# Mixer phase of a hybrid decoder layer: gate rows requested one slice earlier, the last cached weight units kept out of the raw slots, one more slice for the scan

## The chip, the cores and the metric

The kernel runs on one core of a Trainium2 chip, as a single program. Its time is the device time of one execution in microseconds (us), given as the median of several runs. In the profile PE is TensorE (PEld its weight loads), DVE VectorE, ACT ScalarE, POOL GpSimd and SP SyncE; a "q" behind a name is that engine's DMA queue.

## What is computed

One inference step of a decoder layer in float32: a prompt of 2048 tokens and 8 single-token samples, model width 1024. Cut to what matters here:

```python
h = _rmsnorm(x, g_norm1) * (1 + scale1) + shift1
proj = h @ w_in                                  # pool | q k v | z | b a | glu
y_a = _pool_mixer(pool_ext, pos0, pool_w, pool_scale)
qkv = silu(_causal_dwconv(qkv_ext, qkv_conv_w))  # then split; q, k normalised per head
beta = sigmoid(proj[..., OFF_B:OFF_A])
g = -exp(a_log) * softplus(proj[..., OFF_A:OFF_GLU] + dt_bias)
o, s_new = _gated_delta(q, k, v, beta, g, s0)    # chunked: inverse within a chunk, scan over chunks
y_b = rmsnorm(o) * dn_norm_g * silu(z)
y_c = silu(layernorm(_causal_dwconv(glu))) @ conf_pw_w
x = x + gate1 * (concat([y_a, y_b, y_c]) @ w_out)
a = relu((_rmsnorm(x, g_norm2) * (1 + scale2) + shift2) @ w_ff1)
x = x + gate2 * ((a * a) @ w_ff2)                # then a final rmsnorm
```

Returned are the outputs for prompt and samples, and the states of the pool, the two convolutions and the delta rule.

## The kernel before

**Arithmetic.** Matrix products are made from a high and a low part of each operand: `unit_mm` (L172 to 182) adds hi x hi, hi x lo and lo x hi, over eight steps k of 128 rows, so 24 matmuls for one unit (a block of 128 columns of a weight against 512 tokens). The weight's parts are called `whi` and `wlo`, the activation's `hhi` and `hlo`.

**Phases.** First the mixer, then the feed-forward network (L1571 and L1805 are its matmuls). The mixer goes over four groups of 512 tokens. Each group has 22 units of `w_in`, in the order glu (4), pool (2), z0, z1, k (4), v (4), q (4), z2, z3: units 0 to 87 in all. The last group carries the samples too, so that its units are made in two column parts of 260. Behind them come 32 out-projection units, in which the roles are turned: the columns of `y_scr` (the mixer's output, in DRAM) are the weight, and `w_out` is the activation. `load_w` (L1098) fetches its tiles `wt`, casts them to `hhi` on ScalarE (L1109) and subtracts to get `hlo` (`split_lo`, L132) on VectorE or, each few times, on GpSimd.

**Weights.** `load_raw` (L134) fetches a unit into one of two slots with the tag "raw" (L139, on ScalarE's queue). `load_unit` (L142) casts it to `whi` on ScalarE (L151) and makes `wlo` with `split_lo`; both have slots with tags of their own. In group 0 the parts of each `w_in` unit are also written to DRAM (`w_scr`), and in the later groups `load_cached` (L157) only reads both back (L169). Since no raw tile is needed then, every third of these units is put into the two raw slots, in place of a whi and a wlo slot, by a counter `wnum` (L166): unit 86 gets whi and wlo, unit 87 raw and raw. The out-projection units go through `load_unit`. In the job loop (L1303) the weights of a unit are requested three units ahead.

**Delta rule.** For each group, `gates` (L640) computes the decay sums and writes them as rows to `g_scr` (L668); `delta_prep` (L672) reads them back, spread over the partitions, as `Gb` (L678), twice eight heads and chunks, and makes tails and decay matrices from them (L681 to 690). `delta_inverse` solves the triangular systems (L751 and L752 are its substitution on VectorE, L772 its first product). `delta_scan` (L817) does the part within a chunk (`within`, L827 to 830) for two halves, then four chunk steps (`chunk`) and the normalisation (`finish`).

**Order.** These routines are generators: each `yield` ends a slice, and the job loop lets every one that is under way make one slice per unit (`tick`). That is the order in which the program is written. The order on each engine is then made by the framework's scheduler, which takes instructions by priority (program order, moved by `tc.high_priority`) and a simulated time at which they are ready; the slots of a pool decide how early a load can be.

Of the kernel before, what the change touches and what calls it, by code (L numbers as in the profile page):

```python
# [17 lines left out]
P = 128  # L18
# [44 lines left out]
def hybrid_trunk(  # L63
# [13 lines left out]
    w_ada, w_in, w_out, w_ff1, w_ff2 = w_ada[0], w_in[0], w_out[0], w_ff1[0], w_ff2[0]  # L77
# [49 lines left out]
    wcount, lo_share, wnum = [1], [LS], [0]  # L127
# [26 lines left out]

    w_scr = {}

    def load_cached(key, src, early=None):  # L157

        if key not in w_scr:
            hi, lo = load_unit(src, early)  # L160
            w_scr[key] = dram.tile([2, P, D], F32, name=f"w_scr{key}")
            for i, v in enumerate((hi, lo)):
                nc.sync.dma_start(out=w_scr[key][i], in_=v.bitcast(F32).rearrange("p k m -> p (k m)"))
            return hi, lo
        wnum[0] += 1
        tags = (("whi", "wlo"), ("raw", "raw"), ("whi", "wlo"))[wnum[0] % 3]  # L166
        out = tuple(wp.tile([P, KT, P], F32R, tag=t, name=n) for t, n in zip(tags, ("whi", "wlo")))
        for i, v in enumerate(out):
            wq[0].dma_start(out=v.bitcast(F32).rearrange("p k m -> p (k m)"), in_=w_scr[key][i])  # L169
        return out  # L170
# [70 lines left out]
    with ExitStack() as ph1:  # L241
# [26 lines left out]
        early = tc.high_priority(offset=30000)  # L268
# [403 lines left out]
        def delta_prep(g, st):  # L672

            V, A = nc.vector, nc.scalar
            for hf in range(2):
                Gt = st['Gt'][:, hf * 8:hf * 8 + 8]
                Gb = d4.tile([P, 8, P], F32, tag="Gb", name="Gb")
                nc.sync.dma_start(out=Gb, in_=g_scr[g, hf * 8:hf * 8 + 8, :].partition_broadcast(P))  # L678
                eGl = sm.tile([P, 8], F32, tag=f"eGl{hf}", name="eGl")
                tail = sm.tile([P, 8], F32, tag=f"tail{hf}", name="tail")  # L680
                V.tensor_tensor(out=tail, in0=Gb[:, :, P - 1], in1=Gt, op=ALU.subtract)  # L681
                A.activation(out=tail, in_=tail, func=AF.Exp)
                A.activation(out=eGl, in_=Gb[:, :, P - 1], func=AF.Exp)
                QK = d4.tile([P, 8, P], F32, tag="QK", name="QK")
                for i in range(8):
                    V.scalar_tensor_tensor(out=QK[:, i, :], in0=Gb[:, i, :], scalar=Gt[:, i:i + 1], in1=mneg,
                                           op0=ALU.subtract, op1=ALU.min)
                A.activation(out=QK, in_=QK, func=AF.Exp)
                A.activation(out=Gb, in_=Gb, func=AF.Exp)
                st['dec'].append((Gb, QK, eGl, tail))  # L690
                yield
# [125 lines left out]
        def delta_scan(g, st):  # L817
# [61 lines left out]
            within(0)  # L879
            yield  # L880
            within(1)
            chunk(0, 0, osq[0])
            yield
            chunk(0, 1, osq[0])
# [292 lines left out]
        w_ready = [load_cached(c, w_in[:, c:c + P], d4 if i in EARLY else None) for i, c in enumerate(first_jobs)]  # L1177
# [75 lines left out]
        for g in range(NG):  # L1253
            st = {'dec': [], 'inv': []}
# [37 lines left out]
        for q, tiles in OP_PLAN:  # L1292
            jobs.append((None, q, {}, "load_w"))
            for tt in tiles:
# [3 lines left out]
                if tt >= 12 and first_last is None:  # L1298
                    first_last = sum(j[0] is not None for j in jobs)
                jobs.append((y_scr[:, tt * P:(tt + 1) * P], 0, {},  # L1300
                             lambda g, st, pss, tt=tt, q=q, done=done: op_unit(pss[0], tt, q, done)))

        w_jobs = [j[0] for j in jobs if j[0] is not None]  # L1303
        wi = len(w_ready)
        scan = inv = smp = None
        for src, g, st, what in jobs:
            if src is not None:
                if wi == first_last:
                    finish_all(scan)
                if wi < len(w_jobs):  # L1310
                    nxt = w_jobs[wi]
                    w_ready.append(load_cached(nxt, w_in[:, nxt:nxt + P]) if isinstance(nxt, int) else load_unit(nxt))
                    wi += 1
                w = w_ready.pop(0)
                if wi >= len(w_jobs) - len(op_tiles) or wi == len(w_jobs):
# [604 lines left out]
```

## Time and profile before

| | us |
|---|---|
| median of 3 runs (2493.01 to 2502.81) | 2496.91 |
| the profiled execution | 2489.5 |
| its span, from first to last instruction | 2487.8 |
| TensorE busy (94%) | 2340.6 |
| VectorE busy (76%) | 1892.3 |
| ScalarE busy (44%) | 1093.8 |
| GpSimd busy (28%) | 692.1 |
| TensorE's own part of the chain that ended last | 30% of the span |

The page gives busy time by engine; what an engine waited for is in the rows of the timeline, where a bracket holds the idle time before an instruction and what ended it. TensorE's matmuls overlap, so their starts, not their durations, tell the pace: the distance between two starts is what one costs. The granted clock is the share of the full 2.4 GHz that TensorE was given; 0.50 is the lower level, 1.2 GHz.

### The profile page before, as it was taken

What the parts mean: (1) busy time and instruction counts of PE and PEld (TensorE: products, weight loads), DVE (VectorE), ACT (ScalarE), POOL (GpSimd) and SP (SyncE); (2) the same over time, 40 slices, a digit from 0 to 9 for tenths busy, and PEclk for the clock granted to TensorE, in tenths of its full rate; (3) what the DMA queues carried; (4) which work ended last, traced back from release to release, by engine and by line L of the source; (5) the groups of instructions that cost most, each with busy time, mean ns of one, the idle gap of its engine ahead of it and who ended that gap; (6) DMA issues with size and microseconds to landing.
All of it is one profiled execution on the core that took longest, in us unless ns stands there. A gap on an engine that the chain in (4) does not pass through costs nothing. (4 is left out here: it accounts for less than half of the span.)

```text
span 2487.8 us, 36542 instructions
## 1 busy us (share of the span) xinstructions
PE 2340.6 (94%) x12797; PEld 1879.6 (76%) x12797; DVE 1892.3 (76%) x3378; ACT 1093.8 (44%) x2411; POOL 692.1 (28%) x469
## 2 busy tenths in 40 slices
PE   7989999999999999989999999999989999999991
PEld 3567788788999788667777767777668888888881
DVE  3986987887887586677878796767777787777767
ACT  3266247237336443455575675555532221221205
POOL 2101101011111234543237332323431223231324
PEclk9999999999999999999999999999999999999996
DMA  9976434544643567854779785656675555556553
GB/s 328 360 272 223 171 136 163 179 142 158 213 139 124 153 196 222 269 172 132 241 228 333 239 273 171 191 173 185 212 253 163 167 166 167 170 158 180 162 161 146
DMA packets 456327, 490.73 MB, mean 197 GB/s; under 512 B 40106, under 2 KB 364395, under 8 KB 456120
## 3 DMA queue, kind: packets, MB, share of 16 engines
q1 hardware_dynamic: 381296, 386.55, 48.5%
q10 hardware_dynamic: 73088, 96.48, 11.8%
q0 software_dynamic: 1760, 5.38, 0.7%
q8 instruction: 101, 1.65, 0.3%
q14 instruction: 82, 0.67, 0.1%
HBM read 335.63 MB, written 153.07 MB: 196 GB/s over the span
## 5 line engine op out<-in xcount | busy, mean ns | idle before, releaser
L180 PE MATMUL ps_ip<-hhi,whi 128*128 128x512 f32 (+1 forms) x1112 | 410.6, 370 | 11.4 <-ACT whi L151 9.2
L180 PE MATMUL ps_ip<-hhi,wlo 128*128 128x512 f32 (+1 forms) x1112 | 408.7, 368 | 8.4 <-DVE wlo L132 8.1
L180 PE MATMUL ps_ip<-hlo,whi 128*128 128x512 f32 (+1 forms) x1112 | 407.8, 367 | 4.4 <-DVE hlo L132 3.3
L180 PEld LDWEIGHTS ps_ip<-hhi,whi 128*128 128x128 f32 x1112 | 211.0, 190 | 53.2 <-ACT whi L151 10.8
L180 PEld LDWEIGHTS ps_ip<-hhi,wlo 128*128 128x128 f32 x1112 | 210.9, 190 | 48.5 <-DVE wlo L132 12.0
L180 PEld LDWEIGHTS ps_ip<-hlo,whi 128*128 128x128 f32 x1112 | 210.7, 190 | 38.7 <-DVE hlo L132 5.2
L1780 ACT CAST ai<-ai 128x512 fp32r<-128x512 f32 (+1 forms) x128 | 72.3, 567 | 350.0 <-DMA ai<-a_scr 334.4
L1805 PE MATMUL ps_v<-wo,ai 128*128 128x512 f32 x768 | 197.6, 391 | 2.4 <-DVE wo L1399 1.9
L1805 PE MATMUL ps_z<-wo,ai 128*128 128x512 f32 x768 | 197.0, 391 | 2.3 <-DVE wo L1399 1.5
L1805 PE MATMUL ps_x<-wo,ai 128*128 128x512 f32 x768 | 195.3, 395 | 1.7 <-DMA ai<-a_scr 1.7
L1571 PE MATMUL ps_v<-xo,wo 128*128 128x512 f32 x744 | 186.2, 397 | 7.3 <-DVE t L1396 5.2
L552 DVE SCALAR_TENSOR_TENSOR dc<-glu,dww,dc 128x512 f32<-128x512 f32 x240 | 189.3, 816 | 1.7
L1399 DVE TENSOR_TENSOR wo<-s,wo 128x512 fp32r<-128x512 f32 x128 | 122.5, 962 | 84.5 <-ACT wo L1402 83.4
L1571 PE MATMUL ps_x<-xo,wo 128*128 128x512 f32 x744 | 185.5, 397 | 1.0 <-ACT s L1612 0.7
L1571 PE MATMUL ps_z<-xo,wo 128*128 128x512 f32 x744 | 183.2, 394 | 0.3 <-DVE t L1396 0.3
L1402 ACT CAST wo<-raw 128x512 fp32r<-128x512 f32 x192 | 116.5, 619 | 152.3 <-POOL raw L1399 41.1
L1687 POOL TENSOR_TENSOR raw<-raw,g 128x1024 f32<-128x1024 f32 x32 | 84.2, 2653 | 353.1 <-DMA ai<-a_scr 282.6
L1399 DVE TENSOR_TENSOR ai<-ai 128x512 fp32r<-128x512 f32 (+1 forms) x128 | 100.8, 789 | 104.9 <-ACT ai L1780 104.6
L1805 PEld LDWEIGHTS ps_x<-wo,ai 128*128 128x128 f32 x768 | 145.5, 190 | 38.3 <-DVE acc L1396 3.3
L1571 PEld LDWEIGHTS ps_v<-xo,wo 128*128 128x128 f32 x744 | 137.8, 188 | 43.3 <-DVE t L1396 8.0
L1805 PEld LDWEIGHTS ps_z<-wo,ai 128*128 128x128 f32 x768 | 144.3, 188 | 33.8 <-DVE wo L1399 2.3
L1805 PEld LDWEIGHTS ps_v<-wo,ai 128*128 128x128 f32 x768 | 144.2, 188 | 33.6 <-DVE wo L1399 2.9
(507 smaller groups left out, 4774.6 us busy)
## 6 DMA issues: line engine op xcount, KB each, us to landing
a_scr<-ae SPq DMA_DIRECT2D x112, 512.0 KB
raw<-in_w_ff SPq DMA_DIRECT2D x94, 512.0 KB
whi<-w_scr ACTq DMA_DIRECT2D x66, 512.0 KB
wlo<-w_scr ACTq DMA_DIRECT2D x66, 512.0 KB
ai<-a_scr SPq DMA_DIRECT2D x64, 512.0 KB
mraw<-in_w_ada SPq DMA_DIRECT2D x48, 512.0 KB
ai<-a_scr SPq DMA_DIRECT2D x64, 384.0 KB
a_scr<-s SPq DMA_DIRECT2D x80, 256.0 KB
```

Source lines behind the costliest of these rows:

```text
L180: nc.tensor.matmul(out=ps, lhsT=a[:, k, :], rhs=b, start=(i == 0), stop=(i == 3 * KT - 1))
L552: nc.vector.scalar_tensor_tensor(out=d, in0=gt[:, j:j + GT], scalar=dww[:, t, j:j + 1], in1=d, op0=ALU.mult, op1=ALU.add)
L1399: eng.tensor_tensor(out=out, in0=in0, in1=in1, op=ALU.subtract)
L1402: A.copy(out=entry[:, 0, :], in_=full)
L1571: nc.tensor.matmul(out=ps, lhsT=w[:, a, c], rhs=x[:, b, :], start=start and i == 0, stop=stop and i == 2, skip_group_check=True)
L1687: Q.tensor_tensor(out=raw, in0=raw, in1=g2, op=ALU.mult)
L1780: A.copy(out=e[:, :, 0, :], in_=e32[:, :, 1, :])
L1805: nc.tensor.matmul(out=ps, lhsT=a[q][n // 4][:, n % 4, x, :], rhs=w[q][r][:, y, :], start=first and q == 0 and i == 0, stop=last and q == ...
```

## The change

Three edits. (1) `delta_prep` issues both loads of `Gb` in its first slice, ends the slice, and computes from the second slice on; it has three slices now in place of two. (2) `load_cached` takes a flag `last`; with it a unit always takes whi and wlo slots. The job loop sets it for the last two `w_in` units, 86 and 87. (3) `delta_scan` ends a slice between `within(1)` and `chunk(0, 0)`, so that it has one slice more.

```diff
--- before.py
+++ after.py
@@ -154,7 +154,7 @@
 
     w_scr = {}
 
-    def load_cached(key, src, early=None):
+    def load_cached(key, src, early=None, last=False):
 
         if key not in w_scr:
             hi, lo = load_unit(src, early)
@@ -163,7 +163,7 @@
                 nc.sync.dma_start(out=w_scr[key][i], in_=v.bitcast(F32).rearrange("p k m -> p (k m)"))
             return hi, lo
         wnum[0] += 1
-        tags = (("whi", "wlo"), ("raw", "raw"), ("whi", "wlo"))[wnum[0] % 3]
+        tags = (("whi", "wlo"), ("raw", "raw"), ("whi", "wlo"))[0 if last else wnum[0] % 3]
         out = tuple(wp.tile([P, KT, P], F32R, tag=t, name=n) for t, n in zip(tags, ("whi", "wlo")))
         for i, v in enumerate(out):
             wq[0].dma_start(out=v.bitcast(F32).rearrange("p k m -> p (k m)"), in_=w_scr[key][i])
@@ -672,10 +672,14 @@
         def delta_prep(g, st):
 
             V, A = nc.vector, nc.scalar
+            Gbs = []
             for hf in range(2):
-                Gt = st['Gt'][:, hf * 8:hf * 8 + 8]
                 Gb = d4.tile([P, 8, P], F32, tag="Gb", name="Gb")
                 nc.sync.dma_start(out=Gb, in_=g_scr[g, hf * 8:hf * 8 + 8, :].partition_broadcast(P))
+                Gbs.append(Gb)
+            yield
+            for hf, Gb in enumerate(Gbs):
+                Gt = st['Gt'][:, hf * 8:hf * 8 + 8]
                 eGl = sm.tile([P, 8], F32, tag=f"eGl{hf}", name="eGl")
                 tail = sm.tile([P, 8], F32, tag=f"tail{hf}", name="tail")
                 V.tensor_tensor(out=tail, in0=Gb[:, :, P - 1], in1=Gt, op=ALU.subtract)
@@ -879,6 +883,7 @@
             within(0)
             yield
             within(1)
+            yield
             chunk(0, 0, osq[0])
             yield
             chunk(0, 1, osq[0])
@@ -1302,6 +1307,7 @@
 
         w_jobs = [j[0] for j in jobs if j[0] is not None]
         wi = len(w_ready)
+        n_in = sum(isinstance(j, int) for j in w_jobs)
         scan = inv = smp = None
         for src, g, st, what in jobs:
             if src is not None:
@@ -1309,7 +1315,7 @@
                     finish_all(scan)
                 if wi < len(w_jobs):
                     nxt = w_jobs[wi]
-                    w_ready.append(load_cached(nxt, w_in[:, nxt:nxt + P]) if isinstance(nxt, int) else load_unit(nxt))
+                    w_ready.append(load_cached(nxt, w_in[:, nxt:nxt + P], last=wi >= n_in - 2) if isinstance(nxt, int) else load_unit(nxt))
                     wi += 1
                 w = w_ready.pop(0)
                 if wi >= len(w_jobs) - len(op_tiles) or wi == len(w_jobs):
```

In the order that the scheduler makes of it, each engine has the same instructions with the same waits from the start to the q units of the last group; in particular the two loads of `Gb` of each group stand next to each other on SyncE in both kernels. The rows that follow are from the part that differs. Line numbers of the changed kernel are higher by 4 to 6 behind the edits (L719 is L723 there, L903 L908, L905 L910, L1109 L1114).

ScalarE near the end of the q units of group 3, before: the reload of unit 87 (`w_scr_2131` is its copy in DRAM) behind a copy of kT.

```order
L719 COPY kT<-ps_kT 128x512
L169 DMA whi<-w_scr_2131 128x1024
L169 DMA wlo<-w_scr_2131 128x1024
L422 COPY craw<-ps_ip 128x252
L423 ACTIVATE cacc<-ps_ip,cw 128x252
L402 COPY prs<-ps_ip 128x8
```

The same place now, and behind it the place of unit 87's reload:

```order
L723 COPY kT<-ps_kT 128x512
L139 DMA raw<-y_scr 128x8x128
L422 COPY craw<-ps_ip 128x252
L423 ACTIVATE cacc<-ps_ip,cw 128x252
L402 COPY prs<-ps_ip 128x8
L139 DMA raw<-y_scr 128x8x128
```

```order
L398 ACTIVATE th<-cacc 128x512
L723 COPY kT<-ps_kT 128x512
L169 DMA whi<-w_scr_2131 128x1024
L169 DMA wlo<-w_scr_2131 128x1024
L259 ACTIVATE ja,qsq_0_6608<-ps_q 128x128
L422 COPY craw<-ps_ip 128x252
```

The two raw loads of out-projection units 0 and 1 stand where the reload stood, and the reload stands two kT copies further on.

ScalarE behind unit 87, before: the casts of `w_out` (L1109), the raw loads of units 0 and 1, and the cast of unit 0 (L151).

```order
L905 ACTIVATE rows<-ps_rows 3x512
L139 DMA raw<-y_scr 128x8x128 x2
L462 ACTIVATE zg<-ps_ip,dng 128x260
L463 ACTIVATE zth<-ps_ip 128x260
L1109 CAST hhi<-wt 128x512 x2
L469 COPY prs<-zg 128x8
L1109 CAST hhi<-wt 128x512
L151 CAST whi<-raw 128x1024
L1109 CAST hhi<-wt 128x512
L151 CAST whi<-raw 128x1024
```

Now, from behind unit 85 to the raw load of unit 2, and then the casts of `w_out`:

```order
L462 ACTIVATE zg<-ps_ip,dng 128x260
L398 ACTIVATE th<-cacc 128x512
L463 ACTIVATE zth<-ps_ip 128x260
L151 CAST whi<-raw 128x1024
L462 ACTIVATE zg<-ps_ip,dng 128x260
L463 ACTIVATE zth<-ps_ip 128x260
L139 DMA raw<-y_scr 128x8x128
```

```order
L1114 CAST hhi<-wt 128x512
L910 ACTIVATE rows<-ps_rows 3x512
L151 CAST whi<-raw 128x1024
L462 ACTIVATE zg<-ps_ip,dng 128x260
L463 ACTIVATE zth<-ps_ip 128x260
L1114 CAST hhi<-wt 128x512 x2
L910 ACTIVATE rows<-ps_rows 3x512
L139 DMA raw<-y_scr 128x8x128
L1114 CAST hhi<-wt 128x512
L469 COPY prs<-zg 128x8
L1114 CAST hhi<-wt 128x512 x2
```

The cast of unit 0 (the first L151) stands in front of the second zg of unit 86; that of unit 1 between the third and the fourth cast of `w_out`.

TensorE at the passage from unit 87 (128x260) to unit 0 (128x512), before:

```order
L180 MATMUL ps_ip<-hlo,whi 128x260
L180 MATMUL ps_ip<-hhi,wlo 128x260
L903 MATMUL ps_rows<-ident,halo_q 3x128 x4
L903 MATMUL ps_rows<-ident,halo_g 30x128 x2
L180 MATMUL ps_ip<-hhi,whi 128x512
L180 MATMUL ps_ip<-hlo,whi 128x512
L180 MATMUL ps_ip<-hhi,wlo 128x512
```

Now:

```order
L180 MATMUL ps_ip<-hhi,wlo 128x260
L908 MATMUL ps_rows<-ident,halo_q 3x128 x4
L180 MATMUL ps_ip<-hhi,whi 128x260
L180 MATMUL ps_ip<-hlo,whi 128x260
L180 MATMUL ps_ip<-hhi,wlo 128x260
L180 MATMUL ps_ip<-hhi,whi 128x512
L180 MATMUL ps_ip<-hlo,whi 128x512
L180 MATMUL ps_ip<-hhi,wlo 128x512
L180 MATMUL ps_ip<-hhi,whi 128x512
L180 MATMUL ps_ip<-hlo,whi 128x512
L180 MATMUL ps_ip<-hhi,wlo 128x512
L180 MATMUL ps_ip<-hhi,whi 128x512
```

Unit 0 follows unit 87 directly; the transposes of `halo_q` stand inside of it, those of `halo_g` behind it.

## Rows read from the trace of the kernel before

**Rows 1.** From the page: its first line, TensorE's line of busy time (in us, its share of the span, and instructions), and the TensorE clock granted in 40 equal slices of the span, in tenths of full speed.

```profile
span 2487.8 us, 36542 instructions
...
PE 2340.6 (94%) x12797; PEld 1879.6 (76%) x12797; DVE 1892.3 (76%) x3378; ACT 1093.8 (44%) x2411; POOL 692.1 (28%) x469
...
PEclk9999999999999999999999999999999999999996
```

**Rows 2.** The table by stage: window in us and its length, then busy time of PE, PEld, DVE, ACT and POOL, each with its count of instructions, the mean granted TensorE clock, the busy share of the DMA engines, GB/s.

```profile
800.00:826.00 26.00, 26.00 (x224) 25.87 (x223) 15.39 (x41) 15.29 (x61) 3.80 (x2) 1.00 0.31 94
826.00:842.00 16.00, 9.96 (x49) 7.49 (x48) 14.14 (x38) 8.45 (x16) 6.31 (x3) 0.79 0.76 229
842.00:1100.00 258.00, 244.05 (x1468) 198.34 (x1466) 179.53 (x367) 112.74 (x246) 105.66 (x71) 0.99 0.71 220
```

**Rows 3.** The timeline of TensorE between units 87 and out-projection unit 0: start (us), duration (us), engine, line, operation, tiles, and in brackets the idle time before it with what ended it.

```profile
829.34 0.39 PE L903 MATMUL ps_rows<-ident,halo_g 128*30 128x128 f32 x2
835.17 0.79 PE L180 MATMUL ps_ip<-hhi,whi 128*128 128x512 f32 x1 [5.44 <-ACT whi L151]
...
836.95 0.80 PE L180 MATMUL ps_ip<-hhi,wlo 128*128 128x512 f32 x1 [0.56 <-DVE wlo L132]
...
839.25 0.63 PE L180 MATMUL ps_ip<-hlo,whi 128*128 128x512 f32 x1
839.68 0.57 PE L180 MATMUL ps_ip<-hhi,wlo 128*128 128x512 f32 x1
840.09 0.39 PE L180 MATMUL ps_ip<-hhi,whi 128*128 128x512 f32 x1
840.32 0.39 PE L180 MATMUL ps_ip<-hlo,whi 128*128 128x512 f32 x1
```

**Rows 4.** The table by stage for a short stretch, columns as in rows 2.

```profile
835.10:840.00 4.90, 4.26 (x9) 2.97 (x10) 4.80 (x9) 1.98 (x4) 3.73 (x1) 0.50 0.80 257
```

**Rows 5.** The timeline of ScalarE in the same stretch (ACTq: the issue of a DMA from its queue).

```profile
826.81 1.65 ACT L1109 CAST hhi<-wt 128x512 fp32r<-128x512 f32 x3
828.70 0.59 ACT L905 ACTIVATE rows<-ps_rows 3x512 f32<-3x512 f32 x1 [0.24 <-DMA out<-rows]
828.80 1.01 ACTq L139 DMA_DIRECT2D raw<-y_scr  x2
829.86 0.48 ACT L462 ACTIVATE zg<-ps_ip,dng 128x260 f32<-128x260 f32 x1 [0.57 <-PE ps_rows L903]
...
830.50 1.14 ACT L1109 CAST hhi<-wt 128x512 fp32r<-128x512 f32 x2
833.46 0.20 ACT L469 COPY prs<-zg 128x8 f32<-128x8 f32 x1 [1.81 <-DVE zg L465]
833.56 0.61 ACT L1109 CAST hhi<-wt 128x512 fp32r<-128x512 f32 x1
834.08 1.04 ACT L151 CAST whi<-raw 128x1024 fp32r<-128x1024 f32 x1
```

**Rows 6.** What the line of `load_raw` (L139) did from 780 to 1100 us: the time from issue to landing of its loads.

```profile
DMA to landing us min/median/max: 4.9/5.0/5.1
```

**Rows 7.** The timeline of ScalarE somewhat earlier, from the reload of unit 87's cached halves to the end of unit 86.

```profile
805.57 0.33 ACTq L169 DMA_DIRECT2D whi<-w_scr  x1
...
813.50 0.59 ACT L719 COPY kT<-ps_kT 128x512 f32<-128x512 f32 x1 [1.86 <-PE ps_kT L718]
...
821.63 0.48 ACT L462 ACTIVATE zg<-ps_ip,dng 128x260 f32<-128x260 f32 x1 [2.12 <-PE ps_ip L180]
```

**Rows 8.** The timeline of GpSimd about out-projection unit 0.

```profile
826.51 1.31 POOL L132 TENSOR_TENSOR hlo<-wt,hhi 128x512 fp32r<-128x512 f32 x1 [11.01 <-ACT hhi L1109]
...
835.72 3.73 POOL L132 TENSOR_TENSOR hlo<-wt,hhi 128x512 fp32r<-128x512 f32 x1 [5.91 <-DMA wt<-in_w_out]
```

**Rows 9.** What TensorE waited for from 100 to 780 us: operation and line, released by, total us, times, longest.

```profile
PE ps_qk L827 <- DVE QK L829: 5.4, 3, 2.7
PE ps_kv L439 <- ACT swth L518: 5.4, 1, 5.4
```

**Rows 10.** The timeline of TensorE at two later places: the first product of group 3's inverse, and the first feed-forward matmul.

```profile
854.85 1.89 PE L772 MATMUL ps_w<-X,BT 128*128 128x64 f32 x16
...
1099.90 1.22 PE L1571 MATMUL ps<-xo,wo 128*128 128x512 f32 x2 [3.52 <-ACT wo L1402]
```

**Rows 11.** The timeline of SyncE ahead of that product: the loads of the inverse's tile.

```profile
847.57 8.67 SPq L759 DMA_DIRECT2D X<-i_scr  x16
```

**Rows 12.** What TensorE waited for from 842 to 1100 us, columns as in rows 9.

```profile
PE ps_ip L180 <- DVE wlo L132: 6.4, 4, 3.0
```

**Rows 13.** The timeline of VectorE about out-projection unit 0: two steps of the inverse's substitution (L752), of 60 and 55 columns.

```profile
838.33 1.18 DVE L752 TENSOR_TENSOR X<-X,fs 128x60 f32<-128x60 f32 x1
...
839.80 0.22 DVE L752 TENSOR_TENSOR X<-X,fs 128x55 f32<-128x55 f32 x1
```

**Rows 14.** The timeline of all engines about a later out-projection unit.

```profile
986.22 2.92 DVE L119 TENSOR_SCALAR fr_y<-of 128x8 int32<-128x8 int32 x1
...
986.73 2.37 POOL L1062 TENSOR_TENSOR St<-St,ub 128x1024 f32<-128x1024 f32 x1
...
990.32 0.79 PE L180 MATMUL ps_ip<-hhi,wlo 128*128 128x512 f32 x1 [2.99 <-DVE wlo L132]
```

**Rows 15.** The table by stage for the stretch behind it, columns as in rows 2.

```profile
990.30:993.60 3.30, 3.28 (x8) 2.61 (x9) 3.23 (x22) 1.05 (x1) 1.27 (x1) 0.50 0.96 347
```

## The prediction

> **What bounds the kernel now.** I read the page first: TensorE is busy 94% of the span of 2487.8 us at a granted clock of nine tenths or more in nearly every slice [rows 1]. So the time is TensorE's work plus some 147 us in which it stands still, plus the matmuls it runs at the lower of its two clock levels (1.2 instead of 2.4 GHz). A change that alters no matmul can only take from or add to these two. Then I asked where in the mixer the change acts, and read the table by stage: between 826 and 842 us TensorE is busy 9.96 of 16 us at a mean clock of 0.79, while the 26 us before have no idle time at all [rows 2]. The TensorE timeline of that stretch shows one hole: the last transposes of group 3 end at 829.34 + 0.39 = 829.73, and the first out-projection matmul (128x512) starts at 835.17, released by ScalarE's cast of its weights, 5.44 us later; at 836.95 it waits 0.56 more for the low part on VectorE [rows 3]. The clock pays too: in 835.1 to 840.0 the grant is 0.50 and nine matmuls start [rows 4]; the distance of two starts is 0.43 us there (839.25 to 839.68) and 0.23 after it (840.09 to 840.32) [rows 3]. Nine times 0.20 is 1.8 us. The hole costs 5.44 + 0.56 + 1.8 = **7.8 us**.
>
> Why the hole: both raw slots were taken by unit 87 (`z3`, the last projection unit), whose cached halves lie there. Its last matmul frees them at about 828.7, ScalarE issues the two loads of the first out-projection units at 828.80, and the first is cast at 834.08 [rows 5]; a load of this kind takes 4.9 to 5.1 us to land [rows 6]. The order of events is load, cast, matmul, with nothing beside it.
>
> **Part by part: the raw slots.** Units 86 and 87 now always take whi and wlo slots. By the old rotation unit 86 took them already, so one unit changes. From the order of the changed kernel on ScalarE: the two raw loads now stand where unit 87's reload stood, which the trace has at 805.57; unit 87's reload moves two copies of kT further on, behind the one that ends at 813.50 + 0.59 = 814.1 [rows 7]. Two things follow.
>
> (1) Out-projection unit 0 is loaded, cast and split before it is needed. Its cast stands right behind the end of unit 86, which ScalarE sees at 821.63 [rows 7], 7 us ahead of use. This removes the wait for `whi` (5.44) and that for `wlo` (0.56). What is late next: the matmuls of unit 0 need, step by step over k, the eight high and low parts of `w_out` (`hhi`, `hlo`). In the trace four of them are cast by 826.81 + 1.65 = 828.46, two more from 830.50, and then ScalarE stands 1.81 us in front of `prs<-zg` [rows 5]. In the new order three casts come ahead of unit 87's end at about 828.7. After it come: rows 0.59, the cast of unit 1's whi 1.04, zg and zth 0.64, two casts 1.14, rows 0.59, one cast 0.61, prs 0.20, two casts 1.14 [rows 5]. That is 6.0 us, so the last `hhi` is there at about 834.7, its `hlo`, on GpSimd, 1.3 us later (as at 826.51 [rows 8]), and with 0.5 for the last two matmuls unit 0 ends near 836.5. Without any wait TensorE would be there at 835.0: 24 matmuls at 0.23 and two groups of transposes of 0.35 are 6.3 us. In the trace of before the tenth matmul of unit 0 starts at 840.09, and 15 steps of 0.23 with 0.3 for two transposes later, at 843.8, it ended. These transposes and those of `halo_g` (0.3) now stand behind it, so the gain is 843.8 - 0.6 - 836.5 = 6.7. With no wait left it is the whole 7.8. If the last `hlo` comes as late as before (835.72 + 3.73 = 839.45 [rows 8]), unit 0 ends at 840.0 and the gain is 3.2. I take **6**, near the first, since ScalarE's casts pace the unit and the two `wlo` splits beside which that `hlo` took 3.73 are gone from that place; ends 3 and 7.8.
>
> (2) Unit 87's reload is issued some 8.5 us later, at about 814.2. With 5.1 us, what a raw load of this size takes at most [rows 6], and 0.4 for the issue of the second half, it lands at 819.7, and its first matmul comes at about 822, behind unit 86 [rows 7]. Cover: 2 us. The DMA engines are busy 0.31 of 800 to 826 [rows 2], and the raw loads, issued within two us of 805.57, are in before it starts. Cost 0. If the load took twice the 5.1, it would land at 824.8 and cost TensorE 2.8. Ahead of it on ScalarE it waits for unit 85's end; queued behind the wait are unit 85's own copies, which start at that end in the trace as well, so they lose two issues, under 1 us, that nothing on TensorE's path needs.
>
> **The gate rows.** `delta_prep` now issues both Gb loads in its first slice and computes from the second on. In the order of SyncE the two loads of each group are one row of two in both kernels: the scheduler had already put them together. Nor does the order on any engine differ, waits included, from the start to the q units of group 3 (about 805 us). So the waits that look like targets stay: 5.4 us behind `swth`, once, and 5.4 us in three waits on QK [rows 9]. Cost and gain 0; nothing has to hide it.
>
> **The scan's seventh slice.** The extra yield separates `within(1)` from `chunk(0, 0)`. In groups 0 to 2 the order is again the same. In group 3 the scan's instructions follow the inverse, which TensorE first enters at 854.85 [rows 10], long after the slices have been handed out, so data set their time. The scan is finished before the last out-projection tiles need `y_scr`, some twenty units on. Cost 0; if it delays those tiles, the price is one load and one cast in the open, 5.1 + 1.0 us [rows 5, 6].
>
> **The rest of the mixer.** From 805 us on the order of all engines is laid anew up to the first FF1 units; later there are a few small exchanges, and the last 2,600 matmuls stand as before. In 842 to 1100 us TensorE is idle 258 - 244.05 = 14 us [rows 2], 6.4 of them in four waits for `wlo` on VectorE [rows 12], and FF1 begins with 3.52 us of waiting [rows 10]. I expect these to come out alike on average, with some 5 us either way. One place could take the gain back: TensorE arrives 6 us early at the inverse's first product, which needs the loads that SyncE issues from 847.57 on, 16 of them in 8.67 us [rows 11]. The new order puts 22 more matmuls of 0.23 us (5.1 us) ahead of it, which about makes up for it; I take 0 to 1 us.
>
> **Sum.** The profiled execution took 2489.5 us; 2489.5 - 6 = 2483.5. The median of the three runs, 2496.91, lies 7.4 above the profiled one, so the forecast for the median is **2491**.
>
> **The rivals.**
> *The wait moves to hlo.* GpSimd's `hlo` of 3.73 us ran beside VectorE's `wlo`, where the same operation took 1.31 at 826.51; VectorE's L752 next to it took 1.18, and 0.22 a little later [rows 8, 13]. If the split, now beside the inverse's small steps, stays that long, unit 0 ends at 840.0 as worked out above: gain 3, and 1 less if the half clock comes back. Time 2494. For it: the inverse's chain of L751 and L752 still runs on VectorE there; against it: the long `wlo` pair is gone and 826.51 ran beside that chain as well. The Trainium skill, SBUF — State Buffer, "Who interferes with whom", says that a VectorE instruction with two SBUF inputs contends with a GpSimd instruction that reads SBUF; by that rule L752 qualifies too and this rival holds, with 2494. The trace agrees as to a collision, 1.18 against 0.22, but shows it beside the wide `wlo` pair only once. Chance 0.25.
>
> *The new order of the samples' work blocks the splits (slower).* At 990.32 TensorE waits 2.99 for a `wlo`; ahead of it on VectorE stands a small L119 that takes 2.92 beside GpSimd's L1062, and the next 3.3 us run at a clock of 0.50 [rows 14, 15]. One such event costs 2.99 + 7 x 0.20 = 4.4 us. GpSimd and VectorE take the samples' state (L1060 to L1062) and the splits in another sequence now. Two more events than before cancel the gain (2 x 4.4 - 6 = +3, time 2500); past 0.5% it takes five (5 x 4.4 - 6 = 16, time 2513). Against it: before shows only one this long [rows 12]. Chance 0.12, of which 0.05 past 0.5%.
>
> *The tail improves as well.* If the four `wlo` waits and their half clock go too (6.4 + 1.4), and half of the rest, the gain is 6 + 7.8 + 3: time 2480. Chance 0.13.
>
> *The change does all that its words say.* The rows ahead and the new slice would also remove the 5.4 us behind `swth` and the QK waits of 5.4: 6 + 10.8, time 2480, and about 2475 with the clock. The unchanged order up to 805 us speaks against it. Chance 0.03.
>
> **How the numbers follow.** Forecast (gain 4 to 8): 0.47; the five chances add up to 1. The time is that of the likeliest, 2491. The 8 in 10 range takes in the moved wait, the slower case up to one or two blocked splits and most of the better tail, and the scatter of a median of runs that span 2493 to 2503: 2480 to 2502. 0.5% is 12.5 us, about what a measurement of this kernel can tell from no change. Faster by more than that needs the better tail nearly in full (0.10) or the last rival (0.03): 0.13. Slower: 0.05. Within: 0.82.
>
> **What would show it.** Right: the raw loads of the first two out-projection units issue near 806, TensorE's idle time between unit 87 and unit 0 is under 2 us in all, the clock there stays near 1, and unit 87 starts without a wait near 822. Wrong: a hole in front of a 128x512 matmul released by `hlo` or `hhi`; a wait at unit 87's start; waits of 3 us for `wlo` in 950 to 1060 in other number than before; any difference in groups 0 to 2 beyond the scatter, the 5.4 us wait behind `swth` first of all.

## The result, and the profile after

| | us | ratio to before, 95% interval |
|---|---|---|
| before, on the same chip | 2495.49 | |
| changed kernel, median of 4 runs (2512.59 to 2516.72) | 2513.1 | 1.007 (1.0054 to 1.0085) |
| its profiled execution; its span | 2512.89; 2511.2 | |

The forecast was 2491, its range 2480 to 2502. The change costs 0.7%, and the interval lies clear of 1. From the page of the changed kernel, the same lines as in [rows 1]:

```profile
span 2511.2 us, 36560 instructions
...
PE 2351.9 (94%) x12797; PEld 1886.0 (75%) x12797; DVE 1889.0 (75%) x3378; ACT 1091.2 (43%) x2411; POOL 692.1 (28%) x469
...
PEclk9999999999999998989999999999999999999996
```

The span is 23.4 us longer than in [rows 1]. TensorE has the same 12797 matmuls and is busy 11.3 us longer, so these ran at the lower clock for longer; the other 12.1 us are idle time of TensorE. The medians differ by less, 17.6 us: the profiled execution of the kernel before (2489.5) lies 6.0 below its median, that of the changed one 0.2 below, so some 6 of the 23.4 are the scatter of executions. The clock's row shows two of the places, slices 16 and 18 of 40 (942 to 1004 and 1067 to 1130 us): the out-projection, and the passage from its end into the feed-forward phase.

**The hole is gone.** TensorE's timeline of the changed kernel at the passage to the out-projection, to be read beside [rows 3]:

```profile
827.59 0.29 PE L180 MATMUL ps_ip<-hhi,whi 128*128 128x260 f32 x1
...
830.78 0.28 PE L180 MATMUL ps_ip<-hhi,wlo 128*128 128x260 f32 x1
830.90 0.39 PE L180 MATMUL ps_ip<-hhi,whi 128*128 128x512 f32 x1
831.13 0.39 PE L180 MATMUL ps_ip<-hlo,whi 128*128 128x512 f32 x1
...
837.35 0.39 PE L180 MATMUL ps_ip<-hhi,wlo 128*128 128x512 f32 x1
```

No bracket: the first out-projection matmul follows the last of unit 87 after 0.12 us. ScalarE's timeline shows why. The raw loads (L139) are issued at 808 us, where before they came at 828.80 [rows 5]; the reload of unit 87 (L169) stands behind them, and nothing waited for it:

```profile
808.20 0.38 ACTq L139 DMA_DIRECT2D raw<-y_scr  x1
...
808.70 0.82 ACTq L139 DMA_DIRECT2D raw<-y_scr  x1
...
817.08 0.34 ACTq L169 DMA_DIRECT2D whi<-w_scr  x1
817.52 0.39 ACTq L169 DMA_DIRECT2D wlo<-w_scr  x1
...
824.15 1.05 ACT L151 CAST whi<-raw 128x1024 fp32r<-128x1024 f32 x1 [0.62 <-PE ps_ip L180]
```

From the first matmul of unit 87's second column part (827.59) to the 49th of L180 from there (837.35) it is now 9.7 us; in the kernel before the 49th is the first behind unit 0, in the changed one unit 0 ends with it, since the scheduler put one matmul of the next unit ahead. I call this stretch *a*. Two more are compared below: *b* begins where *a* does and ends with the first feed-forward matmul, and *c* goes from there to the 1081st. The table by stage (columns as in rows 2) of the kernel before, with *a*, *b*, *c*:

```profile
825.00:843.80 18.80, 12.77 (x67) 9.75 (x66) 14.14 (x38) 9.28 (x18) 6.31 (x3) 0.82 0.77 234
825.00:1099.90 274.90, 254.91 (x1523) 206.62 (x1522) 193.58 (x405) 121.92 (x264) 111.86 (x74) 0.97 0.72 220
1099.90:1377.60 277.70, 266.14 (x1145) 211.80 (x1146) 221.04 (x286) 162.99 (x279) 115.80 (x76) 0.98 0.70 224
```

And of the changed one:

```profile
827.60:837.30 9.70, 9.70 (x62) 8.23 (x61) 6.15 (x16) 7.76 (x22) 2.61 (x2) 1.00 0.67 190
827.60:1110.80 283.20, 260.33 (x1523) 211.61 (x1521) 191.99 (x406) 121.33 (x270) 110.15 (x74) 0.95 0.69 211
1110.80:1401.70 290.90, 270.10 (x1145) 213.37 (x1146) 219.20 (x285) 161.55 (x278) 115.53 (x76) 0.97 0.67 214
```

*a* fell from 18.8 to 9.7, a gain of 9.1: 6.0 of idle time (18.80 - 12.77) and 3.1 of busy time (12.77 - 9.70; five transposes fewer fall into it, 62 against 67 instructions). But *b*, which contains *a*, grew by 8.3, so that 17.4 were lost in the out-projection behind it, 8.9 as idle time and 8.5 as longer busy time. And *c* grew by 13.2, of which 9.2 idle (290.90 - 270.10 against 277.70 - 266.14). With 2.6 from the part before and -0.7 from all that comes after *c*, this makes up the 23.4. The 2.6 are scatter: TensorE's first 4900 matmuls stand in the same order in both kernels, and the 4900th starts at 809.80 us before and at 812.44 now; over the profiles of the kernels below, in all of which the same 4900 come first, it starts between 807.57 (e11) and 814.38 (e3).

**What took the out-projection's time.** TensorE's waits of the changed kernel from 837.6 to 1111 us (released by; total us, times, longest), to be read beside [rows 12] and the 3.52 of [rows 10]:

```profile
PE ps_ip L180 <- DVE wlo L132: 7.9, 3, 3.8
PE ps L1577 <- ACT wo L1408: 6.4, 1, 6.4
PE ps_rows L908 <- ACT rows L910: 3.5, 1, 3.5
PE ps_ip L180 <- ACT whi L151: 1.9, 2, 1.0
```

Together with smaller ones they make up the 8.9 of added idle time: the waits for `wlo` were 6.4 before, in four, 3.0 at most, and are 7.9 now, in three (1.5 more); the wait for `rows` is new (3.5); that for the first feed-forward weights grew from 3.52 to 6.4 (2.9), and the rest by some 1 us. The longer busy time, 8.5, goes with the granted clock, whose mean behind *a* fell from 0.99 to 0.95. The longest wait for `wlo`, from the timelines of VectorE, GpSimd and TensorE:

```profile
988.42 5.72 DVE L123 SCALAR_TENSOR_TENSOR x_a<-x_a,x1v 128x4 f32<-128x4 f32 x1
...
988.78 2.41 POOL L1067 TENSOR_TENSOR St<-St,ub 128x1024 f32<-128x1024 f32 x1
...
991.72 2.40 POOL L1067 TENSOR_TENSOR St<-St,ub 128x1024 f32<-128x1024 f32 x1
...
995.92 1.22 DVE L132 TENSOR_TENSOR wlo<-raw,whi 128x1024 fp32r<-128x1024 f32 x1
...
997.19 0.79 PE L180 MATMUL ps_ip<-hhi,wlo 128*128 128x512 f32 x1 [3.80 <-DVE wlo L132]
```

A step on four columns holds VectorE for 5.72 us beside the samples' two sums on GpSimd, and the split behind it comes late. This is the event of [rows 14] again, longer. The Trainium skill, SBUF — State Buffer, "Who interferes with whom", has a VectorE instruction with two SBUF inputs contend with a GpSimd instruction that reads SBUF; L123 has two, and the trace agrees: 5.72 us beside the two sums, 0.15 for a step of the same size behind them. The second long wait for `wlo` has a wider step of VectorE ahead of it, beside a split on GpSimd:

```profile
1028.80 2.37 POOL L132 TENSOR_TENSOR wlo<-raw,whi 128x1024 fp32r<-128x1024 f32 x1
...
1029.06 2.67 DVE L1138 TENSOR_TENSOR xres<-xres,gated 128x512 f32<-128x512 f32 x1
...
1031.65 1.21 DVE L132 TENSOR_TENSOR wlo<-raw,whi 128x1024 fp32r<-128x1024 f32 x1
...
1032.92 0.60 PE L180 MATMUL ps_ip<-hhi,wlo 128*128 128x512 f32 x1 [3.58 <-DVE wlo L132]
```

The 3.5 for `rows` is a new wait, from ScalarE's timeline:

```profile
847.08 0.37 ACT L910 ACTIVATE rows<-ps_rows 30x256 f32<-30x256 f32 x1 [4.79 <-DMA out<-rows]
```

ScalarE's waits for these stores were 1.1 us in all in the kernel before (0.24 of them in [rows 5]) and are 9.5 now. ScalarE reaches the next row copy while the store of the last one (3 rows of 512, 6 KB) is still under way. SyncE issued it behind two 512 KB loads of `w_out`:

```profile
839.49 1.04 SPq L1110 DMA_DIRECT2D wt<-in_w_out  x2
841.23 0.28 SPq L911 DMA_DIRECT2D out<-rows  x1
```

### The profile page after: what moved, and what is told of

The parts are those of the page before. It is cut to its first block, busy times and chain, and to the rows that moved or that the text cites. A ratio compares the mean times of both kernels' runs of the same rounds, so it can differ in the third digit from the quotient of the medians.

```text
span 2511.2 us, 36560 instructions
## 1 busy us (share of the span) xinstructions
PE 2351.9 (94%) x12797; PEld 1886.0 (75%) x12797; DVE 1889.0 (75%) x3378; ACT 1091.2 (43%) x2411; POOL 692.1 (28%) x469
## 5 line engine op out<-in xcount | busy, mean ns | idle before, releaser
L180 PE MATMUL ps_ip<-hhi,wlo 128*128 128x512 f32 (+1 forms) x1112 | 411.4, 371 | 8.9 <-DVE wlo L132 8.9
L180 PE MATMUL ps_ip<-hhi,whi 128*128 128x512 f32 (+1 forms) x1112 | 413.3, 372 | 6.7 <-ACT whi L151 4.2
L180 PE MATMUL ps_ip<-hlo,whi 128*128 128x512 f32 (+1 forms) x1112 | 411.3, 370 | 4.4 <-DVE hlo L132 3.3
L180 PEld LDWEIGHTS ps_ip<-hhi,whi 128*128 128x128 f32 x1112 | 212.4, 191 | 49.2 <-ACT whi L151 6.7
L180 PEld LDWEIGHTS ps_ip<-hhi,wlo 128*128 128x128 f32 x1112 | 213.1, 192 | 47.8 <-DVE wlo L132 11.4
L180 PEld LDWEIGHTS ps_ip<-hlo,whi 128*128 128x128 f32 x1112 | 212.7, 191 | 39.7 <-DVE hlo L132 5.2
L1405 DVE TENSOR_TENSOR wo<-raw,wo 128x512 fp32r<-128x512 f32 x192 | 158.7, 834 | 30.5 <-ACT wo L1408 25.6
```

The source lines that it names most:

```text
L180: nc.tensor.matmul(out=ps, lhsT=a[:, k, :], rhs=b, start=(i == 0), stop=(i == 3 * KT - 1))
L1405: eng.tensor_tensor(out=out, in0=in0, in1=in1, op=ALU.subtract)
```

## Experiments

The questions are which edit does it, whether the hole's gain is real, and what takes it back behind *a*. Of the 18 kernels, most come in pairs: the same edit in the changed kernel and in the one before (for the latter at its own line). Medians in us, ratio to the kernel before in the same call; *a*, *b*, *c* from one profile each, by the starts of the same matmuls. The order of TensorE's first 1300 matmuls from the feed-forward start comes out in few forms, by tiles and shapes in the traces; I is that of before, II that of the changed kernel (195 of the 1300 stand elsewhere), each give or take up to 5; III is another. A dash marks an order that is none of these: e5 and e6 differ from II in some 60, e15 and e16 from I in 73 and 42.

| kernel | median | ratio (95%) | a | b | c | order |
|---|---|---|---|---|---|---|
| before | 2495.5 | | 18.8 | 274.9 | 277.7 | I |
| changed | 2513.1 | 1.0070 (1.0054, 1.0085) | 9.7 | 283.2 | 290.9 | II |
| e1 changed, slots alone | 2512.5 | 1.0064 (1.0046, 1.0081) | 9.7 | 281.9 | 290.7 | II |
| e2 rows and slice alone | 2494.0 | 0.9989 (0.9976, 1.0002) | 19.8 | 273.2 | 278.5 | I |
| e3 changed, samples on VectorE | 2513.5 | 1.0059 (1.0043, 1.0075) | 9.8 | 277.6 | 292.9 | II |
| e4 before, same | 2509.6 | 1.0053 (1.0031, 1.0075) | 19.0 | 280.2 | 291.1 | II |
| e5 changed, own rows tiles | 2531.2 | 1.0155 (1.0126, 1.0184) | 9.9 | 279.6 | 306.2 | - |
| e6 before, same | 2529.5 | 1.0145 (1.0118, 1.0172) | 21.9 | 281.2 | 308.6 | - |
| e7 changed, splits on VectorE | 2507.4 | 1.0052 (1.0032, 1.0073) | 9.8 | 280.7 | 285.6 | III |
| e8 before, same | 2507.2 | 1.0052 (1.0033, 1.0070) | 18.9 | 280.3 | 291.8 | II |
| e9 changed, one yield | 2496.1 | 0.9994 (0.9966, 1.0022) | 9.7 | 279.1 | 278.8 | I |
| e10 before, same | 2501.5 | 1.0020 (1.0004, 1.0036) | 19.8 | 276.6 | 279.1 | I |
| e11 before, other FF order | 2513.2 | 1.0080 (1.0062, 1.0098) | 19.9 | 282.7 | 291.9 | II |
| e12 changed, two slices a unit | 2526.4 | 1.0134 (1.0116, 1.0151) | 9.7 | 307.7 | 278.7 | I |
| e13 changed, urgent scan | 2503.3 | 1.0026 (1.0013, 1.0039) | 9.2 | 277.0 | 279.5 | I |
| e14 before, same | 2508.9 | 1.0049 (1.0034, 1.0063) | 20.4 | 289.1 | 278.8 | I |
| e15 changed, late tiles last | 2503.9 | 1.0038 (1.0024, 1.0053) | 9.8 | 274.5 | 289.9 | - |
| e16 before, same | 2503.1 | 1.0024 (1.0011, 1.0037) | 20.8 | 268.5 | 290.1 | - |
| e17 changed, one sum on VectorE | 2494.2 | 1.0002 (0.9991, 1.0014) | 9.8 | 276.3 | 279.7 | I |
| e18 before, same | 2502.6 | 1.0036 (1.0021, 1.0050) | 18.8 | 282.9 | 278.1 | I |

**Which edit?** e1 keeps the flag `last` alone, e2 the other two edits alone.

> The slots of unit 87 alone; the gate rows and the scan's slice as before. The scheduler gives each engine the very order of the changed kernel. If the loss comes from the slots and what the scheduler makes of them: 2513, within 4 us of the changed kernel, with the waits for wlo at about 997 and 1033 us. If one of the other two edits costs it in a way that the order does not show: about 2491.

> The gate rows and the scan's slice alone, unit 87 in the raw slots as before. The order on every engine is that of the kernel before. Theory of the slots: ratio 1.000 within 0.002. If these two edits cost something: 2505 or more.

The slots make the whole difference. In e2 the order of every engine is that of before, in e1 that of the changed kernel.

**Who delays the splits?** e3 and e4 move the samples' state from GpSimd to VectorE, e7 and e8 keep all `split_lo` of the out-projection on VectorE:

```diff
-                Q.tensor_tensor(out=Sv, in0=Sv, in1=ub, op=ALU.add)
+                V.tensor_tensor(out=Sv, in0=Sv, in1=ub, op=ALU.add)
...
+                lo_share[0] = 1 << 30
```

(the first for the three lines L1060 to 1062). e5 and e6 give the row copies two tiles of their own:

```diff
-                t = cv.tile([P, 527], F32, tag="s2", name="rows")[:, 0:512].rearrange("p (a b) -> p a b", a=4)
+                t = cv.tile([P, 512], F32, tag="rows", name="rows", bufs=2)[:, 0:512].rearrange("p (a b) -> p a b", a=4)
```

> The changed kernel with the twelve operations of the samples' state (128x1024 each) on VectorE instead of GpSimd. Theory A (the order behind the hole is laid anew, and there a small VectorE operation stands behind two GpSimd operations of the samples, 5.72 us for one that takes 0.16, in front of a wlo): the wait of 3.80 at 997 us and the half clock behind it go, 7 us; the rest is laid anew: 2500 to 2510. Theory B (unit 87 in a whi and a wlo slot costs by itself, whatever the order behind it): 2513 and some us more, since VectorE has 15 us more to do.

> The same edit in the kernel before. Theory A: its wait of 2.99 at 990 us goes (4 us), the rest is laid anew: 2485 to 2500, and the difference to the changed kernel with this edit need not be 17 us, nor of the same sign. Theory B: 17 us faster than the changed kernel with this edit.

> The changed kernel with two slots of their own for the rows of state that go out (before they share two slots with residual tiles). Theory A: the wait of 3.53 us at 847 us behind these rows is gone with its half clock, 5 us, and the tail is laid anew with an unknown sum of -10 to +10: 2498 to 2518. Theory B: no less than 2508.

> The same edit in the kernel before, where these rows cost TensorE nothing. Theory A: only the new order of the tail counts, 2485 to 2508, and the difference to the changed kernel with this edit is not 17 us. Theory B: 2495, and 17 us less than the changed kernel with this edit.

> The changed kernel with all low parts of the out-projection phase made on VectorE; GpSimd makes none there (10 wlo and 7 hlo fewer). Theory A: the collision at 1029 us (VectorE's addition of 2.67 us beside GpSimd's wlo) is gone, but VectorE has 17 us more: 2500 to 2515. Theory B: 2513 or more.

> The same edit in the kernel before. Theory A: 2485 to 2505, and the difference to the changed kernel with this edit is not 17 us. Theory B: 17 us less than the changed kernel with this edit.

B, that the new slots cost by themselves, whatever the order behind them, falls: with any of these edits in both kernels, the early weights no longer cost 17 us but 3.8, 1.6 and 0.2. A, that the loss lies in the order laid anew behind the hole, had its times no better: of the six only e7's lies in its range, e5 and e6 are 13 and 21.5 us above theirs. *a* is 9 to 12 shorter each time, and *b* differs by -2.6, -1.6 and +0.4. But every one of these kernels is slower than before, with the old slots too: none of these edits, each made against one wait that the trace names, brings the time back. In e3 the waits for `wlo` are down to 1.0 us and in e5 none is left for `rows`, but others stand in their place; in e7 two new ones for `wlo` take 5.2. What the six have in common is *c*: 286 to 309, for either slots.

**Is it the feed-forward order?** e9 and e10 add a `yield` behind the samples' state copy in `samples`; e11 lets the kernel before have one `xres` tile under way instead of two; e12 gives each out-projection unit a second `tick`.

```diff
+            yield
...
-                    while op_tiles and len(xres) < 2:
+                    while op_tiles and len(xres) < 1:
...
+                if src is not None and not isinstance(src, int):
+                    tick()
```

> The changed kernel with one more yield in the samples' routine, behind the copies of its states. TensorE's order is the changed kernel's up to about 910 us; from the first feed-forward matmul on it is word for word that of the kernel before, where the changed kernel has another. Theory C (13 us of the loss are the other order of the feed-forward start): from the first feed-forward matmul to the 1081st it takes 278 us as before, not 291; with the mixer as in the changed kernel the time is 2500, and down to 2488 if its later waits fall better. Theory D (the feed-forward start is slow because the slots or the data come late, whatever the order): 291 us there, 2513.

> The same yield in the kernel before; its feed-forward order stays word for word the same. Theory C: 278 us in that stretch; with a mixer laid anew behind 836 us, 2490 to 2502. Theory D: the same.

> The kernel before, slots as they were, with residual tiles requested one unit ahead and not two. TensorE's order is that of before up to about 910 us, and at the start of the feed-forward network it is that of the changed kernel but for 4 instructions. Theory C: 291 us from the first feed-forward matmul to the 1081st, so 2508, and up to 2515 if the residual tiles come late. Theory D: 278 us there, 2495 to 2502.

> The changed kernel with two slices per out-projection unit for every routine under way. The feed-forward order is that of before but for 4 instructions. Theory C: 278 us in that stretch; the samples' work comes earlier in the mixer: 2490 to 2505. Theory D: 291 us there, 2510 or more.

C, that the order decides, holds both ways, and D, that slots or data come late whatever the order, falls. e9 has the changed slots and order I, and its *c* is 278.8; e11 has the old slots and order II, and its *c* is 291.9 (its *b* grew too, by 7.8). Over all kernels of the table *c* is 277.7 to 279.7 in the nine with order I and 290.7 to 292.9 in the six with order II, and both hold old and new slots. Which of the exchanged matmuls cost the time is not shown: e15 and e16 stand nearer to I, and their *c* is 290. The table by stage of e9, with *b* and *c*:

```profile
826.10:1105.20 279.10, 255.06 (x1523) 207.59 (x1521) 193.40 (x406) 120.58 (x270) 107.79 (x74) 0.97 0.70 214
1105.20:1384.00 278.80, 265.75 (x1145) 211.44 (x1146) 222.15 (x286) 163.13 (x279) 115.41 (x76) 0.98 0.70 223
```

And of e11:

```profile
822.70:1105.40 282.70, 261.88 (x1523) 212.62 (x1521) 194.00 (x405) 123.72 (x265) 114.09 (x74) 0.95 0.70 215
1105.40:1397.30 291.90, 270.06 (x1145) 213.46 (x1146) 219.81 (x285) 160.42 (x276) 114.68 (x75) 0.97 0.66 212
```

The waits that grow in order II are for VectorE's parts of the weights, from the list of waits over *c*, in the changed kernel:

```profile
PE ps_y L1577 <- DVE wo L1405: 6.8, 4, 2.8
...
PE ps_v L1577 <- DVE t L1402: 4.7, 4, 2.3
```

and in e9:

```profile
PE ps_y L1578 <- DVE wo L1406: 3.2, 2, 3.0
...
PE ps_v L1578 <- DVE t L1403: 2.2, 3, 1.4
```

These two rows differ by 6.1 us, of the 7.8 by which the idle time differs between the two (290.90 - 270.10 and 278.80 - 265.75). e12 missed: its *c* was right, 278.7, but two slices a unit pile the delta rule's and the samples' steps on each other, and TensorE waited 14.1 us at one place for GpSimd's `q` and 11.9 at another for VectorE's `gated`.

**What binds the rest of the mixer?** E: its end is set by the chain of inverse, scan and second write of `y_scr`, so that an earlier out-projection gains nothing; F: single waits fall here or there. e13 and e14 step the last group's inverse and scan under `tc.high_priority(offset=300)`; e15 and e16 put the last out-projection tiles, which need that write, four further back; e17 and e18 move only the sum of L1062 to VectorE.

```diff
-                    inv = delta_inverse(g, st)
+                    inv = urgent(delta_inverse(g, st)) if g == NG - 1 else delta_inverse(g, st)
...
-OP_PLAN = [(0, range(8)), (1, range(16)), (0, range(8, 16))]
+OP_PLAN = [(0, range(12)), (1, range(16)), (0, range(12, 16))]
```

> The changed kernel with the inverse and the scan of the last group written at a priority 300 higher. The feed-forward order is that of before but for 4 instructions (278 us in that stretch). Theory E (the mixer's end hangs on the last group's chain inverse, scan, y_scr, and through it on the out-projection units 22 and later, which start at 1026 to 1029 us in every kernel so far, hole or no hole; with early weights unit 0's work on VectorE delays that chain): the chain is shortened, y_scr is written before 1004, unit 22 starts some 6 us earlier than at 1027.9, and from unit 87 to the feed-forward start it takes 268 to 275 us, not 283; time 2482 to 2492. Theory F (the 9 us are given back in waits that fall here or there, no common place): 275 to 285 us in that stretch, 2490 to 2505.

> The same priority in the kernel before; the feed-forward order is that of before but for 4 instructions. Theory E: here too the end hangs on the chain, so the stretch from unit 87 to the feed-forward start is 270 to 275 us against 274.9, and the changed slots with the same priority are not slower than this: 2488 to 2496. Theory F: 270 to 285 us.

> The changed kernel with the out-projection in another order: first half of the columns for tiles 0 to 11, second half for all 16, first half for tiles 12 to 15. The first unit that needs the last group's scan is the 25th and not the 21st, some 24 us later. Theory E: the chain no longer binds, and the hole's 9 us show at the feed-forward start: the stretch from unit 87 to it is 7 to 10 us shorter than with the slots as before and this plan. Theory F: a difference between -5 and +8. The feed-forward order is a third one here (141 of its first 1300 instructions differ from before), so the time itself tells nothing.

> The same plan in the kernel before, with the hole of 5.4 us. Theory E: from unit 87 to the feed-forward start 268 to 276 us, 7 to 10 more than with the changed slots and this plan. Theory F: no such relation.

> The changed kernel with one of the three operations of the samples' state (the sum, four of 128x1024) on VectorE and two left on GpSimd. The feed-forward order is that of before but for 4 instructions. The pair of GpSimd sums behind which the small VectorE operation stood for 5.72 us is gone. Theory F (equal feed-forward orders, the hole's gain against waits that fall here or there): 278 to 280 us in the feed-forward stretch, 272 to 281 from unit 87 to its start: 2485 to 2500. If early weights are worth their 9 us once both collisions are away: 268 to 272 there, 2482 to 2488, faster than both kernels.

> The same in the kernel before; the feed-forward order is word for word that of before. Theory F: 272 to 282 us from unit 87 to the feed-forward start, 2488 to 2500, within 8 us of the changed kernel with this edit either way. If early weights are worth their 9 us: 9 us more than the changed kernel with this edit.

E falls. With the second write of `y_scr` 13.7 us (new slots) and 10.5 us (old) earlier, counted from the start of *a*, *b* shrank by 6.2 with the new slots and grew by 14.2 with the old ones; with the tiles that need it put back, the new slots' *b* should have been 7 to 10 the shorter and was 6.0 the longer. F is what is left of the two, and it explains by saying that nothing common does; its ranges held but for e14, whose *b* of 289.1 lies above 285, and e18, which missed each of them by a little. Over the nine pairs, *b* of the new slots less *b* of the old is +8.3, +8.7 (e1 and e2, the same two orders again), -2.6, -1.6, +0.4, +2.5, -12.1, +6.0 and -6.6: no common sign, and +0.3 on average, where *a* alone is 9 to 12 the shorter in each. So what lies behind *a* is the longer with the new slots, in eight of the nine pairs and by 10 us on average: most of the gain is lost there again. That this is chance, as F has it, is not shown; a common limit other than the chain of E was not tried.

## Why the prediction was wrong

- **The hole, its cause and its end: right**, and its size too small. The raw loads went out at 808, TensorE had no idle time between units 87 and 0, and its clock there stayed at 1.00. Forecast 6, at most 7.8; measured 9.1, of which I count some 0.6 as transposes that only moved behind unit 0. ScalarE's casts and the last `hlo`, for which I had taken off 1 to 2 us, kept nothing waiting, so the rival in which the wait moves to `hlo` did not come (GpSimd's next splits took 1.31 and 1.38 us, not 3.73); and the half clock was worth more than the 1.8 of nine starts.
- **Unit 87's reload at no cost: right.** It was issued at 817.08, 2.9 us later than I had worked out, and no matmul waited.
- **Gate rows and scan slice at no cost: right.** e2 is 0.9989 (0.9976 to 1.0002) of before, with the same order.
- **The first product of the inverse**, for which I took 0 to 1 us, has no wait of its own now; ahead of it stands a new one, of the row transposes ahead of it, 3.53 us at 847.51, behind a store that I had not looked at.
- **The step that failed** is the one that reads "I expect these to come out alike on average, with some 5 us either way", about all that is laid anew behind unit 0. That stretch came out 17.4 us longer up to the first feed-forward matmul, and the place called "a few small exchanges" 13.2 us longer: 30.6 in all, against 9.1 gained. The bound of 5 rested on the waits of the order that was there, which is no bound for another order, and 195 of 1300 matmuls are no few exchanges.
- Of those, the **13 us** are settled: the feed-forward phase begins in order II instead of I, and this is worth 12 to 14 us with the old slots as with the new (e9, e11). It is a side effect of the scheduler, not of the slots: one `yield` elsewhere brings order I and 2496.1 us back.
- The **17 us of the out-projection** are settled in part. The trace names their waits, but not why this order has them where the kernel before has few. The rival of blocked splits came as a mechanism: the events at 997 and 1033 are it, 3.80 and 3.58, with VectorE's step of 5.72 and 2.67 beside GpSimd. That is one event of 3 us more than before, where its sum wanted two to cancel the gain, and all waits for `wlo` together grew by 1.5 of the 8.9 us; the rest came in places that no rival had, the wait for `rows` and the longer one for the first feed-forward weights. Neither a better tail nor an effect of the other two edits came. The collision alone does not decide the time either: e9 has one of 5.69 us on VectorE and a wait of 4.5 for `wlo`, and is as fast as before.
- Each of the eight kernels with the old slots and an edit that changes its order is slower than before by 0.2 to 1.5%. So the order of before is a good one among these, and some of the loss is a lucky draw given up; but some of these edits also give VectorE more to do, and the two were not told apart.
- What the early weights are worth in the whole time stays open. With order I in both kernels of a pair the medians are 5 to 8 us the lower for the new slots (e9 against e10: 2496.1 and 2501.5; e13 against e14: 2503.3 and 2508.9; e17 against e18: 2494.2 and 2502.6), near the 6 of the forecast, though only the last two intervals lie apart. In the pairs with another order, nearly alike in both, they are 1 to 4 us the higher (e3, e5, e15 against e4, e6, e16). None of the 18 kernels is clearly faster than the kernel before.

## What to carry to other kernels

Where a scheduler makes the order, an edit of one slot is two changes: the wait that it removes, whose price the trace shows fairly well (here 6 forecast and 9 us measured), and a new order of all that follows, which the trace of the old order does not price. Compare the order up to the very end, and take as the bound of a re-laid stretch the scatter between several small edits (here 278 to 309 us for one stretch of the feed-forward phase), not the waits that stand there now. To judge such an edit, make it in pairs: with and without it, under two or three other small edits. And since one profile is one execution, compare its span with the median first (here up to 12 us apart, e10).

## What was not expected of the hardware

A VectorE instruction on 128x4 elements took 5.72 us, where its neighbour of the same size (L124, 994.33) took 0.15: it began 0.36 us before the first of two GpSimd sums of 2.4 us and ended at 994.14, when the second had ended at 994.12. Between the two sums GpSimd issued a DMA, from 991.13 on, and VectorE did not come free there either. With the samples' state on VectorE (e3, e4), no VectorE step on 128x4 or 128x8 elements between 830 and 1110 us took more than 2.4 us; in e9, e8 and e10, where those sums are on GpSimd, one took 5.69, 7.04 and 7.16, and as in the changed kernel it ended within 0.1 us of the end of a run of GpSimd's instructions. And a store of 6 KB, issued at 841.23 behind two loads of 512 KB, released its tile only at 847.08, 5.85 us later, and ScalarE stood 4.79 us in front of the copy behind it.

The granted clock differed between executions of the same instructions: in the kernel before TensorE stood idle for 2.66 us at 312 us, and the clock stayed at 1.00; in e16 the same place, 2.74 us idle, was followed by a stretch at 0.50.
